# One level of Strassen's algorithm in the up-projections of three feed-forwards

## The chip, the cores and the metric

One NeuronCore of a Trainium2 chip runs the whole program. The metric is device time in microseconds (us). The kernel before takes 2163.91 us (median of 3 runs, 2163.86 to 2165.43).

## The reference, cut to what matters

Three decoder layers run over 512 tokens of 1024 features: a gated linear recurrence (HGRN2), dilated attention, and a sparse attention beside gated linear attention. Each is followed by the same kind of feed-forward, with an inner width of 22 times 128. Everything is float32.

```python
def swiglu_ffn(u, w_in, w_down):
    gate, up = jnp.split(u @ w_in, 2, axis=-1)
    return (jax.nn.silu(gate) * up) @ w_down
...
        h = h + swiglu_ffn(rmsnorm(h, norm_ffn[layer]), ffn_w_in[layer], ffn_w_down[layer])
```

## The kernel before, in words

Activations lie feature-major: a tile is 128 features by 512 tokens. To keep float32 accuracy with fast products, every operand is split into a head (the value rounded to float32r) and a rest (value minus head), and a product of two operands is three matmuls: rest by head, head by head, head by rest (`mm3`, L387). Each matmul loads its own 128x128 stationary weights and streams 512 tokens.

A feed-forward (`ffn`, L1421) runs in two halves of 11 column pairs. A pair is one 128-column tile of the gate matrix and one of the up matrix; `gemm` (L407) makes each tile as 8 blocks of the inner dimension by three matmuls. `evac_up` takes the bank of a gate tile through VectorE (times the norm factor `r_bc`), ScalarE (Silu) and GpSimd (times `r_bc` again), and the bank of an up tile through VectorE (times the gate), ScalarE and VectorE (`split`, L525, into head and rest `h`). After 11 pairs the down-projection runs over those 11 tiles, into 8 output tiles that are added to the residual `x`; then the second half does the same, and in its down-projection `norm_feed` (L449) builds the operands of the next norm.

The norm's factor is computed late: `norm_stats` (L483) and `norm_bc` (L518) wait in a list of hooks, and `tile_end` (L377) runs one of them at each of the first two tile ends of the next product, while `evac` calls are held back.

Weights come as units of 1024 columns (8 blocks). `Weights` (L240) has 3 raw buffers and 3 pairs for heads and rests. `load` (L282) issues a 512 KB DMA on SyncE's queue, `heads` (L262) casts on ScalarE, `rests` (L273) subtracts, on GpSimd for odd units and on VectorE for even ones. `take` (L291) hands blocks to the products, issues heads at 3/8 of a unit and rests at 5/8, so a unit is ready about 1.4 to 1.6 units ahead.

Engines work through their queues in program order, so the order of the calls is the order of the work on each engine. The tile framework gives a new tile a buffer of its pool that was freed earlier, and its first writer waits for the last reader of the tile that held it. `Clock` (L163) only decides where background steps of the mixers are put.

`finish` (L1457) makes the last output tile of the program in two halves of 256 tokens, with the same three matmuls per block, each with its own weights. This is the only long stretch of the kernel before that streams 256 columns per matmul.

Of the kernel before, what the change touches and what calls it, by code (L numbers as in the profile page):

```python
# [17 lines left out]
KD = 8  # L18
FF = 22
# [5 lines left out]
# columns of the packed per-feature vectors  # L25
# [10 lines left out]
# columns of the constants that stay  # L36
# [16 lines left out]
def nsa_rows():  # L53
    """Feature order of the NSA heads: tile j holds head j of group 0 and head j of group 1."""
    return np.concatenate([np.arange((e * 4 + j) * 64, (e * 4 + j) * 64 + 64) for j in range(4) for e in range(2)])


def attn_heads():
    """(head of the group, group) in the order in which the output projection takes them."""
    return [(t, g) for t in range(4) for g in (1, 2)] + [(t, 0) for t in range(4)]  # L60


def weight_plan():
    """The order in which weight blocks are used: (section, [(matrix, k tile, columns)])."""
# [14 lines left out]
    def ffn(name_in, name_down, name_up=None):  # L79
        out = []  # L80
        for half in range(2):
            tiles = []
            for i in range(FH):
                tiles.append(cols((half * FH + i) * 128))
                tiles.append(cols(FF * 128 + (half * FH + i) * 128))
            out += fm(name_in, range(KD), tiles, 2 if half == 0 else 1)
            out += fm(name_down, range(half * FH, half * FH + FH), [cols(m * 128) for m in range(8)], 2)
        return out
# [9 lines left out]
    plan.append(("hgrn", c))  # L98
# [8 lines left out]
    plan.append(("attn", c))  # L107
# [26 lines left out]
    plan.append(("blk2", c))  # L134
# [4 lines left out]
def plan_units(sec, chunks):  # L139
    """Cut a section's blocks into units of at most UNIT columns; the first ones are small, to start early."""  # L140
# [22 lines left out]
class Clock:  # L163
    """Rough times of the engines' queues and of the tiles' contents while the program is laid out:
    they say when a background step's inputs and banks will be there, so that TensorE isn't made to wait."""

    def __init__(self, hop):
        self.hop = hop  # from an instruction's end to the start of another engine's that waits for it
        self.free = {"pe": 0.0, "v": 0.0, "a": 0.0, "g": 0.0}
        self.written, self.read = {}, {}  # L170
        self.held = []
# [4 lines left out]
    def banks(self, now):  # L176
        """PSUM banks that are free by then."""
# [62 lines left out]
class Weights:  # L240
    """Streams the weights in the order of use and splits each into its float32r head and rest."""

    RAW, SPLIT = 3, 3

    def __init__(self, prog, ctx, aps):
        tc = prog.tc
        self.nc, self.v, self.a, self.g = tc.nc, prog.v, prog.a, prog.g
        self.raw_p = ctx.enter_context(tc.tile_pool(name="w_raw", bufs=self.RAW))
        self.sp_p = ctx.enter_context(tc.tile_pool(name="w_split", bufs=self.SPLIT))
        self.units = []  # L250
        for sec, chunks in weight_plan():
            off = 0
            for cur, w in plan_units(sec, chunks):
                ap = aps[sec][off:off + 128 * w].rearrange("(p n) -> p n", p=128)
                self.units.append((ap, [len(c[2]) for c in cur], w))
                off += 128 * w
        self.n_dma = self.n_head = self.n_rest = 0
        self.raw, self.split = {}, {}
        self.at, self.pos, self.idx = 0, 0, 0
        self.look = 1  # L260

    def heads(self, look):  # L262
        while self.n_head < min(self.at + look, len(self.units)):
            u = self.n_head
            self.load(u + 1)
            w = self.units[u][2]
            hi = self.sp_p.tile([128, UNIT], F32R, name="w_hi", tag="w_hi")
            lo = self.sp_p.tile([128, UNIT], F32R, name="w_lo", tag="w_lo")
            self.a.copy(hi[:, :w], self.raw[u][:, :w])
            self.split[u] = (hi, lo)  # L270
            self.n_head += 1

    def rests(self):  # L273
        while self.n_rest < self.n_head:
            u = self.n_rest
            w = self.units[u][2]
            hi, lo = self.split[u]
            (self.g if u % 2 else self.v).tensor_sub(lo[:, :w], self.raw.pop(u)[:, :w], hi[:, :w].bitcast(F32))
            self.n_rest += 1
        self.load(self.n_rest + self.RAW - 1)  # L280

    def load(self, n):  # L282
        while self.n_dma < min(n, len(self.units)):
            u = self.n_dma
            ap, _, w = self.units[u]
            raw = self.raw_p.tile([128, UNIT], F32, name="w_raw", tag="w_raw")
            self.nc.sync.dma_start(raw[:, :w], ap)
            self.raw[u] = raw
            self.n_dma += 1

    def take(self, n):  # L291
        ap, widths, w = self.units[self.at]
        if self.idx == 0:
            self.split.pop(self.at - 1, None)
            if self.at not in self.split:
                self.heads(1)
                self.rests()
        if self.idx == 3 * len(widths) // 8:
            self.heads(self.look)
        if self.idx == 5 * len(widths) // 8:  # L300
            self.rests()
        assert widths[self.idx] == n, (self.at, self.idx, widths, n)
        hi, lo = self.split[self.at]
# [3 lines left out]
        if self.idx == len(widths):  # L307
            self.at, self.idx, self.pos = self.at + 1, 0, 0
        return r


class Program:
# [74 lines left out]
    def mm3(self, out, a, b, first, last):  # L387
        """out += a^T b for operands given as (head, rest)."""
# [18 lines left out]
    def gemm(self, xs, M, evac, lead=1, ms=None):  # L407
# [15 lines left out]
    def gemm_tok(self, n, residue=False, before=None, after=None, every=1):  # L423
        """Token-major product with n weight columns: four banks of 128 tokens, by blocks or by the rest of the token mod 4."""
# [24 lines left out]
    def norm_feed(self, k, squares=True):  # L449
        """x[k] is final: build the operand's parts and add its squares."""  # L450
# [25 lines left out]
    def sums(self, out, acc, residue=False):  # L476
        """Each token's sum over the partitions of acc, onto the token's partition."""
# [1174 lines left out]
```

## Time and profile before

| | |
|---|---|
| median of 3 runs | 2163.91 us |
| profiled execution, span of its instructions | 2162.1 us |
| profiled execution, own time | span and about 1.8 us around it, 2163.9 us |
| mean granted TensorE clock | 0.994 of full speed |
| TensorE busy | 2117.4 us, 98% of the span |
| VectorE, ScalarE, GpSimd busy | 46%, 36%, 33% |
| DMA, mean | 88 GB/s |

A profile line gives the start in us, the duration, the engine (PE is TensorE, PEld its weight loads, DVE VectorE, ACT ScalarE, POOL GpSimd, SP SyncE), the operation and its tiles as out<-in. Nearly all operations are recorded at line L228, the timing wrapper, so groups are told apart by tile names. Busy spans of PE overlap, since matmuls are pipelined: the pace of a stretch is read from the distance of starts. "[... <-X]" is idle time of the engine just before and what ended it.

### The profile page before, as it was taken

Reading aid. Unit: us, or ns where it says so; the run is one execution under the profiler, and the core shown is the slowest. Engines: PE = TensorE matmul, PEld = TensorE weight load, DVE = VectorE, ACT = ScalarE, POOL = GpSimd, SP = SyncE. Lnnn points to the kernel's source line nnn. Section 1 sums busy time; section 2 is a strip of 40 time slices with the busy share of each in tenths; the row PEclk is TensorE's granted clock in tenths of the full one; section 3 lists DMA queues with packets and bytes.
Section 4 is the critical chain, followed back from the end, with each engine's and each line's share of the span. In section 5 each row is a group of like instructions: output and inputs, shape, how many; then the busy total and the mean of one; then the engine's idle time right before and its main releaser. Section 6 shows DMA issues by size and latency. Waiting matters only on the chain.

```text
span 2162.1 us, 25412 instructions
## 1 busy us (share of the span) xinstructions
PE 2117.4 (98%) x9983; PEld 1773.4 (82%) x9983; DVE 1004.3 (46%) x1775; ACT 783.8 (36%) x1290; POOL 723.6 (33%) x442
## 2 busy tenths in 40 slices
PE   9999999999999999999999999999899999999998
PEld 7787788888888998788888888887688788888887
DVE  4778853322334555643322333447778753222322
ACT  5343443222233433443222224244455543222233
POOL 4413343323333434323322335331511253322333
PEclk9999999999999999999999999999999999999999
DMA  5111233323323222222332232321111223333332
GB/s 178 59 59 49 69 127 98 98 98 98 98 88 107 79 88 78 79 69 98 98 102 93 98 98 92 133 69 48 55 55 57 70 95 98 98 98 98 96 100 69
DMA packets 55865, 191.00 MB, mean 88 GB/s; under 512 B 6257, under 2 KB 8321, under 8 KB 55745
## 3 DMA queue, kind: packets, MB, share of 16 engines
q1 hardware_dynamic: 53584, 183.85, 26.2%
q0 software_dynamic: 1008, 3.42, 0.4%
q10 hardware_dynamic: 1152, 2.10, 0.3%
q8 instruction: 78, 1.28, 0.2%
q14 instruction: 43, 0.34, 0.1%
HBM read 187.25 MB, written 2.10 MB: 88 GB/s over the span
## 4 chain that ended last, share of the span: by engine, by line
PE 86%; DVE 9%; issue 1%; POOL 1%; ACT 1%; DMA 1%; SPq 0%; DVEq 0%; ACTq 0%; POOLq 0%
PE ps L228 86%; DVE Q L228 2%; DVE Sd L228 2%; DVE P L228 1%; DMA w_raw<-in_hgrn 1%; DVE w_lo L228 1%; DVE K L228 0%; POOL rot L228 0%; DVE Pc L228 0%; DVE qs L228 0%; POOL rs L228 0%; DVE obl L228 0%; DVE GQ L228 0%; DVE PT L228 0%; POOL w_lo L228 0%
## 5 line engine op out<-in xcount | busy, mean ns | idle before, releaser
L228 PE MATMUL ps<-u,w_hi 128*128 128x512 f32 x3392 | 1049.4, 391 | 0.0
L228 PEld LDWEIGHTS ps<-u,w_hi 128*128 128x128 f32 x3392 | 638.9, 188 | 128.9 <-issue 1.4
L228 PE MATMUL ps<-u,w_lo 128*128 128x512 f32 x1696 | 683.7, 403 | 2.2 <-POOL w_lo L228 2.2
L228 POOL TENSOR_TENSOR w_lo<-w_raw,w_hi 128x1024 fp32r<-128x1024 f32 (+2 forms) x173 | 415.8, 2403 | 745.1 <-ACT w_hi L228 636.2
L228 ACT CAST w_hi<-w_raw 128x1024 fp32r<-128x1024 f32 (+2 forms) x346 | 356.1, 1030 | 301.6 <-PE ps L228 205.4
L228 PEld LDWEIGHTS ps<-u,w_lo 128*128 128x128 f32 x1696 | 319.7, 189 | 68.3 <-issue 4.2
L228 PE MATMUL ps<-h,w_hi 128*128 128x512 f32 (+1 forms) x1078 | 326.3, 385 | 0.0
L228 DVE TENSOR_TENSOR w_lo<-w_raw,w_hi 128x1024 fp32r<-128x1024 f32 (+2 forms) x173 | 231.5, 1338 | 183.7 <-ACT w_hi L228 175.4
L228 PEld LDWEIGHTS ps<-h,w_hi 128*128 128x128 f32 x1078 | 200.9, 188 | 40.4
L228 PE MATMUL ps<-h,w_lo 128*128 128x512 f32 (+1 forms) x539 | 207.6, 385 | 0.5 <-DVE x L228 0.5
L228 POOL TENSOR_TENSOR sg<-sg,r_bc 128x512 f32<-128x512 f32 x66 | 85.8, 1299 | 290.3 <-ACT sg L228 290.3
L228 DVE TENSOR_TENSOR x<-x,ps 128x512 f32<-128x512 f32 (+1 forms) x73 | 49.5, 678 | 218.6 <-PE ps L228 218.6
L228 PE MATMUL ps<-w_hi,u 128*128 128x512 f32 (+1 forms) x448 | 139.1, 392 | 2.3 <-DVE u L228 2.3
L228 DVE TENSOR_TENSOR h<-ps,sg 128x512 f32<-128x512 f32 x66 | 45.7, 692 | 194.9 <-PE ps L228 182.4
L228 ACT ACTIVATE sg<-gs 128x512 f32<-128x512 f32 x66 | 41.7, 632 | 242.3 <-DVE gs L228 242.3
L228 ACT CAST h<-h 128x512 fp32r<-128x512 f32 x66 | 41.0, 620 | 242.8 <-DVE h L228 242.8
L228 DVE TENSOR_TENSOR gs<-ps,r_bc 128x512 f32<-128x512 f32 x66 | 45.6, 691 | 156.8 <-PE ps L228 156.7
L228 PEld LDWEIGHTS ps<-h,w_lo 128*128 128x128 f32 x539 | 101.2, 188 | 20.9 <-DVE x L228 0.7
L228 ACT ACTIVATE P<-P,nm 128x128 f32<-128x128 f32 (+2 forms) x112 | 55.2, 494 | 142.6 <-DVE nm L228 130.4
L228 POOL TENSOR_TENSOR sq_acc<-sq_acc,sq 128x512 f32<-128x512 f32 x48 | 67.2, 1405 | 117.8 <-ACT sq L228 115.7
L228 PEld LDWEIGHTS ps<-w_hi,u 128*128 128x128 f32 x448 | 95.0, 226 | 10.3 <-DVE u L228 2.7
L228 PE MATMUL ps<-w_lo,u 128*128 128x512 f32 (+1 forms) x224 | 85.8, 383 | 0.0
(294 smaller groups left out, 2231.5 us busy)
## 6 DMA issues: line engine op xcount, KB each, us to landing
w_raw<-in_ffn SPq DMA_DIRECT2D x198, 512.0 KB, 3.5
w_raw<-in_attn SPq DMA_DIRECT2D x48, 512.0 KB, 3.5
w_raw<-in_blk SPq DMA_DIRECT2D x47, 512.0 KB, 3.4
w_raw<-in_hgrn SPq DMA_DIRECT2D x36, 512.0 KB, 3.5
w_raw<-in_blk SPq DMA_DIRECT2D x7, 404.0 KB, 2.9
x<-in_xt SPq DMA_DIRECT2D x8, 256.0 KB, 5.1
w_raw<-in_hgrn SPq DMA_DIRECT2D x8, 256.0 KB, 4.0
x<-in_xt ACTq DMA_DIRECT2D x8, 256.0 KB, 5.0
```

What stands on the lines that cost most here:

```text
L228: r = f(*args, **kw)
```

## The change

In each feed-forward the first 5 column pairs (FC) are made as before; the other 17 by one level of Strassen's algorithm (6 in the first half, 11 in the second). The 2x2 blocks are: the inner dimension in even and odd k tiles, the columns in gate and up tile, the tokens in two halves of 256. Seven products a1, b1, a2, b2, c, a3, a4 replace eight; each is 4 inner blocks by three matmuls of 256 columns. Their order interleaves neighbouring pairs: a4 of a pair comes after a1 and b1 of the next.

Of the activations, `strassen_operands` makes sums and splits for two k tiles at a time, four times in a feed-forward, during the first 5 pairs (VectorE and ScalarE). Of the weights, each pair needs four sums of 512 columns on VectorE, heads on ScalarE and rests on VectorE; two of the rests (half of the third tile and that of a4) are made by ScalarE writing the negated head and a GpSimd-issued DMA adding the weights to it from memory. All weight tiles share one pool of 12 buffers of 4 KB. Ordinary units get the heads 8.8 and the rests 7.5 us ahead by a planned clock; in the feed-forwards their rests are all on VectorE. The two norm hooks run at k = 4 and 6 of the first group of tiles. The scratch for software DMA descriptors goes from the default to 4096 bytes.

```diff
+FC = 5
+REST = {"hgrn": "vg", "ffn0": "v", "attn": "vg", "ffn1": "v", "blk2": "vg", "ffn2": "v"}
+S_AT = {"a1": 0, "b1": 1, "a2": 3, "b2": 4, "c": 5, "a3": 6, "a4": 9}
+S_LAST = {"a1": 0, "b1": 1, "a2": 3, "b2": 4, "a3": 5, "c": 6, "a4": 7}
+def strassen_order(n):
+    at = [(7 * g + t, g, p) for g in range(n) for p, t in (S_AT if g < n - 1 else S_LAST).items()]
+    return [(g, p) for _, g, p in sorted(at)]
...
-    RAW, SPLIT = 3, 3
+    ROOM, HELD = 12, 3
+    TILE, SLOT = 0.68, 1.44
...
+        self.pool = ctx.enter_context(tc.tile_pool(name="w", bufs=self.ROOM))
...
+    def rest_dma(self, lo, hi, ap):
+        self.a.activation(lo, hi.bitcast(F32), AF.Copy, scale=-1.0)
+        self.nc.gpsimd.dma_start(lo, ap, accum_op=ALU.add)
+
+    def group(self, grp):
...
+        def sums_1():
+            add("r1", second, "r4", second, "r4", first)
+            add("r3", second, "r1", first, "r4", second)
+        def sums_2():
+            t["r2"] = self.tile(F32)
+            add("r2", first, "r1", first, "r1", second)
+            add("r2", second, "r3", first, "r2", first)
+        def heads(i):
+            def go():
+                t["h%d" % i] = self.tile()
+                self.a.copy(t["h%d" % i][:, :2 * n], t["r%d" % i][:, :2 * n])
...
+        def rests(i):
+            def go():
+                h, l = t["h%d" % i], self.tile()
...
+                if i == 3:
+                    self.rest_dma(l[:, first], h[:, first], aps[2])
+                    self.sub(v, l[:, second], t["r3"][:, second], h[:, second])
+                else:
+                    self.sub(v, l[:, :2 * n], t["r%d" % i][:, :2 * n], h[:, :2 * n])
+                self.free(t, "r%d" % i)
...
+        def last():
+            t["l4"] = self.tile()
+            hi, lo = t["l4"][:, second], t["l4"][:, first]
+            self.a.copy(hi, t["r4"][:, first])
+            self.rest_dma(lo, hi, aps[0][:, first])
...
+        for use, lead, what in (
+            ("a1", 7, sums_1), ("a1", 6, sums_2), ("a1", 5, heads(1)), ("a1", 4, rests(1)), ("a2", 6, heads(2)), ("a2", 5, rests(2)),
+            ("c", 6, heads(3)), ("c", 5.9, rests(3)), ("a1", 0, last),
+        ):
+            self.todo.append((at[use] - lead * s + 0.01, u, what, len(self.loads)))
...
+            while self.n_load < len(self.loads) and self.live < self.ROOM - self.HELD:
+                self.load(self.n_load + 1)
...
+                if grp[0] == 0 and k in hooks_at:
+                    self.hooks.popleft()()
...
+    def strassen_operands(self, k, gain):
+        B1, B2, t13, t24 = [self.s2("E", (128, 2, 256)) for _ in range(4)]
+        for B, i in ((B1, k), (B2, k + 1)):
+            v.scalar_tensor_tensor(
+                B.rearrange("p a n -> p (a n)"), self.x[i], gain[:, i:i + 1], self.r_bc, op0=ALU.mult, op1=ALU.mult)
+        v.tensor_sub(t13[:, 0], B1[:, 0], B1[:, 1])
+        v.tensor_sub(t13[:, 1], B2[:, 1], B1[:, 1])
+        v.scalar_tensor_tensor(t24[:, 0], t13[:, 0], -1.0, B2[:, 1], op0=ALU.mult, op1=ALU.subtract)
+        v.scalar_tensor_tensor(t24[:, 1], t24[:, 0], -1.0, B2[:, 0], op0=ALU.mult, op1=ALU.subtract)
+        for src, names in ((B1[:, 0:1], ("a1",)), (t13, ("b1", "a3")), (B2, ("c", "b2")), (t24, ("a2", "a4"))):
...
+            a.copy(P[:, 0], src)
+            v.tensor_sub(P[:, 1], src, P[:, 0].bitcast(F32))
...
+            if i in (1, 2, 4, 6):
+                X.append(self.strassen_operands(2 * len(X), self.V[inner]))
...
+            def c(ps):
+                v.tensor_add(gt[:, n1], gt[:, n1], ps)
+                a.activation(gt[:, n1], gt[:, n1], AF.Silu)
+            def b2(ps):
+                v.tensor_add(gt[:, n2], gt[:, n2], ps)
+                a.activation(gt[:, n2], gt[:, n2], AF.Silu)
+            def a3(ps):
+                v.tensor_add(f[:, n2], f[:, n2], ps)
+                v.scalar_tensor_tensor(f[:, n2], f[:, n2], -1.0, gt[:, n2], op0=ALU.mult, op1=ALU.mult)
+            def a4(ps):
+                v.scalar_tensor_tensor(f[:, n1], ps, -1.0, gt[:, n1], op0=ALU.mult, op1=ALU.mult)
+                hh[i] = self.split(f, "h")
+            return {
+                "a1": lambda ps: a.copy(gt[:, n1], ps), "b1": lambda ps: a.copy(f[:, n2], ps),
+                "a2": lambda ps: a.copy(gt[:, n2], ps), "b2": b2, "c": c, "a3": a3, "a4": a4,
...
-    nc = bacc.Bacc("TRN2", target_bir_lowering=False, num_devices=1)
+    nc = bacc.Bacc("TRN2", target_bir_lowering=False, num_devices=1, dynamic_dma_scratch_size=4096)
```

## Rows read from the trace of the kernel before

**Rows 1.** The page's head and its busy time of each engine.

```profile
span 2162.1 us, 25412 instructions
...
PE 2117.4 (98%) x9983; PEld 1773.4 (82%) x9983; DVE 1004.3 (46%) x1775; ACT 783.8 (36%) x1290; POOL 723.6 (33%) x442
```

**Rows 2.** The chain of work that ended last, by engine.

```profile
PE 86%; DVE 9%; issue 1%; POOL 1%; ACT 1%; DMA 1%; SPq 0%; DVEq 0%; ACTq 0%; POOLq 0%
```

**Rows 3.** Busy time in stretches: the first feed-forward's up, down, up, down.

```profile
core 0: us, PE busy (x) PEld busy (x) DVE busy (x) ACT busy (x) POOL busy (x), PEclk, DMA share, GB/s
319.00:439.60 120.60, 120.60 (x537) 99.76 (x536) 39.07 (x48) 38.27 (x48) 41.63 (x23) 1.00 0.30 96
439.60:499.50 59.90, 59.90 (x266) 49.57 (x265) 13.36 (x15) 12.12 (x12) 11.97 (x5) 1.00 0.32 105
499.50:619.20 119.70, 119.70 (x530) 99.12 (x529) 38.50 (x43) 34.07 (x43) 40.61 (x22) 1.00 0.29 93
619.20:679.00 59.80, 59.80 (x266) 49.51 (x265) 20.17 (x21) 20.39 (x26) 24.02 (x13) 1.00 0.30 95
```

**Rows 4.** Timeline of PE at the program's end: 512, then 256 columns per matmul.

```profile
2140.81 0.39 PE L228 MATMUL ps<-h,w_lo 128*128 128x512 f32 x1
...
2141.49 0.39 PE L228 MATMUL ps<-h,w_lo 128*128 128x512 f32 x1
...
2142.88 0.28 PE L228 MATMUL ps<-h,w_lo 128*128 128x256 f32 x1
...
2143.24 0.28 PE L228 MATMUL ps<-h,w_lo 128*128 128x256 f32 x1
```

**Rows 5.** Groups by shape on DVE and ACT, whole span: busy, mean ns.

```profile
L228 DVE SCALAR_TENSOR_TENSOR x<-x,vec,ps 128x512 f32<-128x512 f32 x8 | 5.6, 741 | 0.0
...
L228 DVE TENSOR_TENSOR x<-x,ps 128x256 f32<-128x256 f32 x2 | 0.8, 420 | 3.9 <-PE ps L228 3.9
...
L228 ACT ACTIVATE sq<-x 128x256 f32<-128x256 f32 x2 | 0.8, 417 | 3.8 <-DVE x L228 3.8
...
L228 ACT COPY r_bc<-ps 128x256 f32<-128x256 f32 x2 | 0.7, 373 | 2.2 <-PE ps L228 2.2
```

**Rows 6.** Groups by shape in one up-projection, 499.5 to 619.2 us.

```profile
L228 ACT CAST w_hi<-w_raw 128x1024 fp32r<-128x1024 f32 x22 | 22.9, 1040 | 4.3 <-PE ps L228 4.3
L228 DVE TENSOR_TENSOR w_lo<-w_raw,w_hi 128x1024 fp32r<-128x1024 f32 x11 | 16.4, 1487 | 18.0 <-ACT w_hi L228 18.0
...
L228 DVE TENSOR_TENSOR gs<-ps,r_bc 128x512 f32<-128x512 f32 x11 | 7.6, 692 | 37.7 <-PE ps L228 37.7
...
L228 DVE TENSOR_TENSOR h<-h 128x512 fp32r<-128x512 f32 x10 | 6.9, 693 | 6.9 <-ACT h L228 6.9
...
L228 ACT CAST h<-h 128x512 fp32r<-128x512 f32 x10 | 6.2, 620 | 39.4 <-DVE h L228 39.4
```

**Rows 7.** Timeline of the same stretch: a rest on DVE beside POOL, and alone.

```profile
604.47 1.30 POOL L228 TENSOR_TENSOR sg<-sg,r_bc 128x512 f32<-128x512 f32 x1 [1.98 <-ACT sg L228]
605.36 1.49 DVE L228 TENSOR_TENSOR w_lo<-w_raw,w_hi 128x1024 fp32r<-128x1024 f32 x1 [1.64 <-ACT w_hi L228]
...
625.92 1.22 DVE L228 TENSOR_TENSOR w_lo<-w_raw,w_hi 128x1024 fp32r<-128x1024 f32 x1 [4.43 <-ACT w_hi L228]
```

**Rows 8.** DMA issues, whole span: size, median us from issue to landing.

```profile
w_raw<-in_ffn SPq DMA_DIRECT2D x198, 512.0 KB, 3.5
...
tab<-in_rope POOLq DMA_DIRECT2D x2, 256.0 KB, 4.6
...
cosr<-in_rope POOLq DMA_DIRECT2D x1, 256.0 KB, 5.2
```

**Rows 9.** DMA issues from 1350 to 1370 us, where both queues are busy.

```profile
w<-in_w POOLq DMA_DIRECT2D x4, 512.0 KB, 7.9
w_raw<-in_blk SPq DMA_DIRECT2D x2, 512.0 KB, 5.8
```

**Rows 10.** Timeline of DVE and ACT in the norm hooks of the first feed-forward.

```profile
330.48 0.69 DVE L228 TENSOR_REDUCE st<-ps 128x4 f32<-128x512 f32 x1 [7.15 <-PE ps L228]
331.53 0.18 DVE L228 RECIPROCAL r<-rt 128x4 f32<-128x4 f32 x1 [0.36 <-ACT rt L228]
...
331.20 0.30 ACT L228 ACTIVATE rt<-st,eps 128x4 f32<-128x4 f32 x1 [4.21 <-DVE st L228]
```

More of the change, by code (lines that the diff above doesn't have):

```diff
@@ new lines, in __init__, with plain, load, heads @@
+        self.todo.sort(key=lambda x: x[0])
+        self.n_todo = self.n_load = 0
+        self.at, self.pos, self.idx, self.now = 0, 0, 0, 0.0
+        self.look = 1
+    def plain(self, ap, widths, w, use, rest):
+        unit = {"ap": ap, "widths": widths, "w": w, "use": use}
+        u = len(self.units)
+        self.units.append(("c", unit, None))
+        def load():
+            unit["raw"] = self.tile(F32)
+            self.nc.sync.dma_start(unit["raw"][:, :w], ap)
+        def heads():
+            unit["hi"] = self.tile()
+            self.a.copy(unit["hi"][:, :w], unit["raw"][:, :w])
+        def rests():
+            unit["lo"] = self.tile()
+            hi, lo = unit["hi"][:, :w], unit["lo"][:, :w]
+            if rest == "d":
+                self.rest_dma(lo, hi, ap)
+            else:
+                self.sub(self.g if rest == "g" else self.v, lo, unit["raw"][:, :w], hi)
+            self.free(unit, "raw")
+        self.loads.append([load, u])
+        self.todo.append((use - 8.8, u, heads, len(self.loads)))
+        self.todo.append((use - 7.5, u, rests, len(self.loads)))
@@ new lines, in tile, with free, advance @@
+    def tile(self, dt=F32R):
+        self.live += 1
+        assert self.live <= self.ROOM, (self.at, self.now)
+        return self.pool.tile([128, UNIT], dt, name="w_raw" if dt == F32 else "w", tag="w")
+    def free(self, tiles, *names):
+        for n in names:
+            del tiles[n]
+            self.live -= 1
+    def load(self, n):
+        while self.n_load < min(n, len(self.loads)):
+            self.loads[self.n_load][0]()
+            self.n_load += 1
+    def advance(self):
+        while self.n_todo < len(self.todo):
+            due, u, what, n = self.todo[self.n_todo]
+            if due > self.now or (self.look == 1 and u > self.at):
+                break
+            self.load(n)
+            what()
+            self.n_todo += 1
+        if self.look > 1:
+            while self.n_load < len(self.loads) and self.live < self.ROOM - self.HELD:
+                self.load(self.n_load + 1)
@@ L304, in take @@
+    def take(self, n):
+        _, unit, _ = self.units[self.at]
+        self.now = max(self.now, unit["use"] + self.pos / 128 * self.TILE)
+        self.advance()
+        hi, lo = unit["hi"], unit["lo"]
+        assert unit["widths"][self.idx] == n
         r = hi[:, self.pos:self.pos + n], lo[:, self.pos:self.pos + n]
@@ L306, in take, with product @@
         self.pos += n
-        if self.idx == len(widths):
+        if self.idx == len(unit["widths"]):
             self.at, self.idx, self.pos = self.at + 1, 0, 0
+            self.free(unit, "hi", "lo")
+        return r
+    def product(self, p):
+        _, grp, name = self.units[self.at]
+        assert p == name, (self.at, p, name)
+        self.now = grp["at"][p]
+        self.advance()
+        r = grp["split"].pop(p)
+        self.at += 1
+        if p in ("b1", "b2", "a3", "a4"):
+            self.free(grp["tiles"], *{"b1": ("l1", "h1"), "b2": ("l2", "h2"), "a3": ("l3", "h3"), "a4": ("l4",)}[p])
         return r
@@ new lines, in strassen @@
+    def strassen(self, X, afters):
+        banks = {}
+        for g, p in strassen_order(len(afters)):
+            key = g, p[0]
+            first = key not in banks
+            if first:
+                banks[key] = self.ps((128, 256))
+            hi, lo = self.W.product(p)
+            for j in range(len(X)):
+                sl = slice(128 * j, 128 * j + 128)
+                self.mm3(banks[key], (hi[:, sl], lo[:, sl]), X[j][p], first and j == 0, j == len(X) - 1)
+            afters[g][p](banks[key])
@@ L1450, in ffn @@
             last = half == 1 and not operands
-            self.gemm(hh, 7 if last else 8, evac_dn, lead=2)
+            self.gemm(hh[mine], 7 if last else 8, evac_dn, lead=2)
+            if not last:
+                hh[mine] = [None] * FH
         if last:
-            self.finish(hh)
+            self.finish(hh[mine])
         else:
```

198 lines of the change are left out of this document (114 added, 84 removed).

## The prediction

> **What bounds the kernel now.** I read the page's head first: of a span of 2162.1 us TensorE is busy 98%, the other engines 33 to 46% [rows 1]. The chain that ended last agrees: 86% of it is PE, 9% DVE, everything else 1% or less [rows 2]. So the first question is how much TensorE time goes, and the second whether the helpers can still feed it. The change sits in the feed-forwards, so I read the first one by stretches: up 120.6, down 59.9, up 119.7, down 59.8 us, 360.0 in all. In each PE is busy for the whole stretch at a granted clock of 1.00, the level of 2.4 GHz [rows 3]. DVE works 38.5 of the 119.7 us of an up-projection there, ACT 34.1, POOL 40.6: a third each, with two thirds idle to be filled.
>
> PE's pace I read from starts, since busy spans overlap. In the timeline of the program's end three matmuls of 512 columns go by from 2140.81 to 2141.49, 0.68 us, and three of 256 columns from 2142.88 to 2143.24, 0.36 us [rows 4]. Each has its own 128x128 weights in both cases. A matmul of half the columns costs 0.120 us, 53% of 0.227.
>
> **PE's term.** A pair takes 16 blocks before (2 tiles of 8), 16 x 0.68 = 10.88 us; 11 pairs make 119.7, which is the stretch [rows 3]. After it takes 7 products of 4 inner blocks, 28 x 0.36 = 10.08 us. That is 0.80 saved, not the 1.36 of an eighth, because of the 53%. Three feed-forwards have 51 such pairs: **-40.8 us**, if PE never waits for its operands. Unchanged are the down-projections, the 5 plain pairs (5 x 10.88 = 54.4 us), the mixers.
>
> One rule of the Trainium skill gives another size. Its page "TensorE: Matmul & The Clock Gate", section "Back-to-back issue gap", has 109 ns for 256 columns and 216 ns for 512. By these a pair would go from 10.37 to 9.17 us, -61 us in 51 pairs. The rows' 120 and 227 ns decide; no row here shows 109.
>
> **What it asks of the other engines.** Per Strassen pair, 10.08 us of PE:
> - DVE: four sums of 512 columns, priced by the two-operand subtraction of a split, 0.69 [rows 6]: 2.76. Rests: two of 1024 columns at 1.22, the time without POOL beside it [rows 7], and half of one, 0.69: 3.13. Evacuation: five operations on 256 columns at 0.42 [rows 5] and the rest of the split, 0.69: 2.79. In all **8.7 us, 86%**.
> - ACT: three heads of 1024 at 1.04 and three half-size operations (one negation for l3, head and negation for a4, 256 columns each, 0.37): 4.2. Evacuation: three copies at 0.37, two Silus at 0.42 (priced as the square), one head of the split 0.62 [rows 5, 6]: 2.6. In all **6.8 us, 67%**.
> - POOL only issues the adding DMAs. The two multiplications by `r_bc` of a pair and its share of the rests are gone from it.
> - DMA: 1024 KB per pair as before, plus two adding DMAs that read 256 KB each again, so half as much again on a share of 0.30 [rows 3]. Mean bandwidth is no bound.
>
> So the engines fit by their sums, but DVE only by 1.4 us per pair, and queues are in order: what counts is the chains that cross between them.
>
> **The first 5 pairs.** In these 54.4 us DVE has the gate and up evacuation of 5 pairs, 5 x (0.69 + 0.74 + 0.69) = 10.6; all 10 or 11 rests, x 1.22 = 13.4; four times `strassen_operands`: 2 x 0.74 to scale, 4 x 0.42 for the sums, about 0.42 + 3 x 0.69 for the rests, 5.2, so 21; the sums and rests of the first Strassen pairs about 6; the hooks' 2 [rows 5, 6, 7, 10]. Some 53 of 54.4 us: nearly full, so now and then late. Bounds: 0, if the 7.5 us of lead take it all, and 6 us a feed-forward, one `strassen_operands` with its hop, that PE waits in full. I take 1 us each, nearer to the lower end since weight rests lead: **+3** (0 to 18).
>
> **The chain of the weights.** A pair's own chain runs through three queues. Load of r4 3.5 us [rows 8], four sums 2.8, then on DVE and ACT in turn heads and rests for tiles 1 to 3, with the evacuations of earlier products queued between them: `c`'s and `b2`'s adds and Silus, a4's 0.42, the split. If each step finds its engine free it starts 7 slots of 1.44 us ahead of a1 and all is hidden. It does not always: an add that waits for a bank stands before the next rest, and the rest for ACT's head. I add up the order in which one pair's steps stand: a4's add 0.42, split head 0.62, head 1.04, rest 1.22, b2's add 0.42, Silu 0.42, head 1.04, rest 1.22, four sums 2.76, about **9.2 us**. That is inside 10.08, spare 0.9. The trace of before has no such loop, so I bound its waits by these rows: 0 per pair, if it turns inside 10.08; about 2.5, if a load of 3.5 comes into it (below). I take 0.35, nearer to the lower end, since the loop without a load fits: 0.35 x 51 = **+18**.
>
> **The adding DMAs.** No row has one. The nearest are plain POOL-queue loads of 256 KB, 4.6 and 5.2 us to landing [rows 8], and 512 KB ones where both queues are busy, 7.9, beside which a 512 KB SP load takes 5.8 in place of 3.5 [rows 9]. The tight one is the third tile's for `c`: its head is due 6 products (8.64 us) before `c`, behind the Silu of the pair before. Add and Silu 0.84, head 1.04, negation 0.37 to 0.62, hops 0.2, then 4.6 to 5.2: 7.1 to 7.9 us, hidden with some 0.7 to 1.5 to spare. With 7.9 to landing it is 10.4, PE waits about 2 us in each pair. An accumulation also reads its target, so below the plain load it can't be, above it can. I take 5, **0**; both ends stay in the range. A page of the Trainium skill, "DMA: Bandwidth & Descriptors", section "Anatomy of one DMA — SWDGE", prices such a transfer at 2.0 us and its bytes at 436 GB/s, 2.6 us by my estimate; the rows' 4.6 and 5.2 stand against it, and by either the term is 0.
>
> **The rest.** Rests only on DVE take nothing from PE in the plain stretches: 1.22 against a unit of 5.4 us (8 x 0.68). The hooks at k = 4 and 6 are two inner blocks of two tiles apart, 4 x 0.68 = 2.7 us; the chain between them is reduce 0.69, root 0.30, reciprocal 0.18 with hops, 330.48 to 331.71 [rows 10]: **0**. The heads' and rests' new leads (8.8 and 7.5 us) in the mixers are about the 1.4 to 1.6 units of before: **0**; bounds one rest of 1.2 us sooner or later in each of the three mixers, -4 to +4.
>
> **Sum.** Profiled execution: span 2162.1 and 1.8 around it, 2163.9, as the median of 2163.91. 2163.9 - 40.8 + 3 + 18 + 0 = **2144 us**.
>
> **The rivals.**
> *All hidden.* Loop and DMAs stay inside 10.08 us: 2123, with small stage losses 2118 to 2130. For it: sums of 86 and 67%, a loop of 9.2. Against: 0.9 us of spare over three in-order queues. Chance 0.24.
> *A load in the loop (slower).* All weight tiles share 12 buffers, so r4's load, the first of a pair, waits for whatever buffer was freed first. If that is the one of r2, freed by the second rest of the pair before, the load's 3.5 us stand in the loop: 9.2 + 3.5 = 12.7, or 2.6 more than PE needs, in some 45 pairs +117, 2164 - 41 + 117 = 2240. It decides from 0.8 us of wait a pair upward: there the whole saving is gone. Where only half of it shows, 2180 to 2200. Against: heads and rests read by PE are freed earlier in part. Chance 0.15.
> *The adding DMA lands late (slower).* At 7.9 us, +2 x 51 = +102 on 2123: 2225; at 7.0, about +1 x 51: 2174. Chance 0.14.
> *The matmuls don't shrink.* If weights did not load under 256 columns, a matmul would take twice its 0.12. [rows 4] has them back to back with own weights, so 2 x 84 x 0.12 = 20.2 us a pair, +9.3 x 51 = +474, 2638: chance 0.01. The Trainium skill ("TensorE: Matmul & The Clock Gate", section "LDWEIGHTS") has a load at 107 ns for 128 columns; this row shows it hidden.
> *No change within 0.2%* (2159.6 to 2168.2, about what a measurement of this kernel can tell): waits of 0.8 a pair by chance: 0.08.
>
> **How the numbers follow.** Forecast, waits of 0.1 to 0.7 us a pair, 2130 to 2159: 0.38. With all hidden, 0.24: faster 0.62. Same 0.08. Slower 0.15 + 0.14 + 0.01 = 0.30. The likeliest case's own range is 2130 to 2159; to hold 8 in 10 it reaches down to 2119 and up to 2195, which leaves out the upper half of the slower cases.
>
> **What would show it.** In the second Strassen stretch of a feed-forward (11 pairs) the profile should take 111 us if PE never waits, 115 by my forecast, 120 at break-even, 139 with a load in the loop. Starts of 256-column matmuls 0.12 us apart; DVE 85% busy, ACT 67%, POOL near 0. Idle PE before `a1` or `a2` ended by a rest on DVE shows the loop; before `c` or `a4`, ended by a DMA, the adding ones; waits of SP on a buffer before r4's load, the pool. It is wrong if the stretch takes 111 and the time still doesn't fall (then the plain pairs lose it), or if 256-column matmuls start further apart than 0.12 with nothing to wait for.

## The result and the profile after

The changed kernel takes **2247.84 us** (median of 4 runs, 2243.74 to 2255.88) against 2164.43 before on the same chip: a ratio of 1.0391 (95% interval 1.0371 to 1.0410). It is slower by 83 us; the forecast was 2144 and the range ended at 2195.

The page's head and busy times, to be held against [rows 1]:

```profile
span 2242.0 us, 30605 instructions
...
PE 2114.1 (94%) x11819; PEld 1844.4 (82%) x11819; DVE 1358.9 (61%) x2402; ACT 999.9 (45%) x1750; POOL 507.0 (23%) x394
```

The span is 79.9 us longer, while PE's busy time is about what it was (2117.4). No engine became full: DVE went from 46% to 61%. So PE waits. Where, the windows of the first feed-forward tell, cut as in [rows 3] but with the up-projection's plain and Strassen pairs apart; the last line is the end of the second Strassen stretch alone:

```profile
core 0: us, PE busy (x) PEld busy (x) DVE busy (x) ACT busy (x) POOL busy (x), PEclk, DMA share, GB/s
319.40:378.07 58.67, 56.43 (x249) 45.41 (x248) 47.87 (x73) 27.25 (x40) 7.87 (x5) 1.00 0.19 59
378.07:456.25 78.18, 66.27 (x505) 64.84 (x505) 48.22 (x75) 41.29 (x73) 11.61 (x13) 0.94 0.58 145
456.25:516.18 59.93, 59.93 (x266) 49.64 (x265) 23.39 (x27) 13.69 (x14) 0.86 (x1) 1.00 0.25 72
516.18:644.84 128.66, 115.84 (x926) 113.30 (x925) 84.49 (x135) 72.61 (x129) 18.21 (x21) 0.97 0.61 146
644.84:704.70 59.86, 59.86 (x266) 49.55 (x265) 25.87 (x26) 20.05 (x26) 11.69 (x9) 1.00 0.31 100
640.10:644.84 4.74, 4.74 (x25) 4.74 (x26) 1.56 (x2) 0.42 (x1) 0.00 (x0) 0.58 0.30 88
```

The down-projections are as before. Six Strassen pairs take 78.18 us where PE needs 60.5 (6 x 10.08), eleven take 128.66 where it needs 110.9; before, eleven pairs took 119.7. The three feed-forwards together are 73.8 us longer, the three mixers 6.1.

What PE waited for in the whole span (us in total, times, longest), the first lines:

```profile
PE ps L249 <- DMA w<-in_ffn: 57.8, 39, 6.8
PE ps L249 <- ACT G L249: 15.0, 12, 2.6
```

And the timeline of PE in the second stretch:

```profile
568.06 10.46 PE L249 MATMUL ps<-E,w 128*128 128x256 f32 x84 [0.48 <-DMA w<-in_ffn]
579.23 10.33 PE L249 MATMUL ps<-E,w 128*128 128x256 f32 x84 [0.71 <-DMA w<-in_ffn]
...
622.79 11.81 PE L249 MATMUL ps<-E,w 128*128 128x256 f32 x96 [0.64 <-DMA w<-in_ffn]
640.10 4.90 PE L249 MATMUL ps<-E,w 128*128 128x256 f32 x24 [5.50 <-DMA w<-in_ffn]
644.84 1.55 PE L249 MATMUL ps<-h,w 128*128 128x512 f32 x6
```

Two things are to be seen. In the **middle**, PE runs 84 matmuls (one pair) and then waits half a microsecond for an adding DMA, pair after pair: 10.8 to 11.2 us from one start to the next, against 10.88 for a plain pair. So the whole saving is gone. At the **end** of the stretch it waits 5.50 us, and the last 24 matmuls (c and a4) then take 4.74 us in place of 2.88: the granted clock there is 0.58, between the levels of 2.4 and 1.2 GHz (1.00 and 0.50), while the pairs of the middle, 568.06 to 622.79 us, ran at 1.00. All six stretches end so: waits of 5.5 to 6.8 us, 36.2 in all, and then 4.5 to 5.3 us for the last 24 matmuls, 12.4 more than at full clock.

The profile names the DMA as the releaser. Whether it is the cause is another question: what comes last is not always what sets the pace. By the prediction's own list of signs (idle PE before `c`, ended by a DMA) it would be the adding DMAs.

### The profile page after: what moved, and what is told of

It reads as the page before. It is cut to its first block, busy times and chain, and to the rows that moved or that the text cites. A ratio compares the mean times of both kernels' runs of the same rounds, so it can differ in the third digit from the quotient of the medians.

```text
span 2242.0 us, 30605 instructions
## 1 busy us (share of the span) xinstructions
PE 2114.1 (94%) x11819; PEld 1844.4 (82%) x11819; DVE 1358.9 (61%) x2402; ACT 999.9 (45%) x1750; POOL 507.0 (23%) x394
## 5 line engine op out<-in xcount | busy, mean ns | idle before, releaser
L249 PE MATMUL ps<-u,w 128*128 128x512 f32 x2640 | 664.3, 401 | 8.1 <-DVE w L249 7.3
L249 PE MATMUL ps<-E,w 128*128 128x256 f32 x4284 | 546.8, 290 | 74.6 <-DMA w<-in_ffn 57.8
L249 PEld LDWEIGHTS ps<-E,w 128*128 128x128 f32 x4284 | 534.0, 197 | 88.0 <-DMA w<-in_ffn 66.3
L249 PEld LDWEIGHTS ps<-u,w 128*128 128x128 f32 x2640 | 485.7, 189 | 111.9 <-DVE w L249 10.7
L249 ACT CAST w<-w_raw 128x1024 fp32r<-128x1024 f32 (+2 forms) x448 | 438.5, 984 | 224.6 <-DVE w L249 113.4
L249 DVE TENSOR_TENSOR w<-w_raw,w 128x1024 fp32r<-128x1024 f32 (+2 forms) x323 | 386.9, 1200 | 205.9 <-ACT w L249 158.9
L249 PE MATMUL ps<-h,w 128*128 128x512 f32 (+1 forms) x1617 | 361.6, 385 | 0.5 <-DVE x L249 0.5
L249 PEld LDWEIGHTS ps<-h,w 128*128 128x128 f32 x1617 | 299.4, 188 | 60.9 <-DVE x L249 0.7
L249 POOL TENSOR_TENSOR w<-w_raw,w 128x1024 fp32r<-128x1024 f32 (+3 forms) x74 | 176.3, 2383 | 371.8 <-ACT w L249 288.7
L249 DVE TENSOR_TENSOR w_raw<-w_raw 128x512 f32<-128x512 f32 x204 | 135.5, 688 | 49.2 <-DMA w_raw<-in_ffn 47.6
L249 PE MATMUL ps<-w,u 128*128 128x512 f32 (+1 forms) x672 | 156.7, 389 | 1.8 <-DVE u L249 1.8
```

What stands on the lines that cost most here:

```text
L249: r = f(*args, **kw)
```

## The experiments

The first four took the adding DMAs away, all or in part, since theory A (the adding DMAs are the loss) is what the list of waits says.

**Both by POOL (e1), c's alone (e2), a4's alone (e3).** e1 has both edits, e2 the first, e3 the second:

```diff
-                    self.rest_dma(l[:, first], h[:, first], aps[2])
+                    self.sub(self.g, l[:, first], t["r3"][:, first], h[:, first])
...
-            self.rest_dma(lo, hi, aps[0][:, first])
+            self.sub(self.g, lo, t["r4"][:, first], hi)
```

> Both adding DMAs of a pair (the third tile's for c, and a4's) become a subtraction on POOL; nothing else changes. Theory A (the adding DMAs are the loss: each pair c waits for its own, and at the end of each half two of them meet the loads of the down-projection): the 57.8 us that PE waits for DMA w go, and with them the low clock behind the long waits, some 20 us. Time 2165 (2155 to 2178); stretch of 11 Strassen pairs 112 to 116 us in place of 128.7. Rival B (the loop over DVE and ACT is too long by itself, or a load waits for a buffer in it): the DMA waits turn into waits for DVE w or ACT w, stretch 122 to 128, time 2215 to 2248. Rival C (POOL beside DVE slows DVE, rests of 1.22 become 1.49): stretch 116 to 120, time 2175 to 2200.

> Only c's adding DMA becomes a subtraction on POOL; a4's stays a DMA. Theory A, with the loss in c's loop: the waits in the middle of a stretch (0.5 to 0.7 us a pair) go, and at the end of a half a4's DMA alone lands 1 to 2 us late: time 2175 (2165 to 2190). Rival A2 (the queue is simply overloaded, any adding DMA makes waits): 2200 to 2230. Rival B: 2215 to 2248.

> Only a4's adding DMA becomes a subtraction on POOL; c's stays a DMA. Theory A, with the loss in c's loop: the steady waits stay at 0.4 to 0.7 a pair, and at the ends c's DMA is alone in its queue and lands 2 to 3 us earlier: time 2230 (2215 to 2240). Rival A2 (two transfers crowd the queue): half or more of the loss goes, 2180 to 2205. Rival B: 2240 to 2248.

Measured: e1 2223.51 (1.0277, 1.0262 to 1.0293), e2 2206.99 (1.0199, 1.0182 to 1.0216), e3 2235.37 (1.0334, 1.0319 to 1.0350). Without any adding DMA the kernel (e1) is still 60 us slower than before, so theory A alone fell; the time is in rival B's range. e2 was a miss for theory A too: its time is in the range of rival A2, but not for A2's reason, since PE's waits for a DMA are down to 6.5 us and it waits 42.2 us for ACT's G. e3 came out as theory A said: c's waits stay (44.1 us for DMA w), the ends get shorter. e1 is worse than e2 for a reason of its own, in its timeline:

```profile
567.47 2.73 POOL L249 TENSOR_TENSOR w<-w_raw,w 128x512 fp32r<-128x512 f32 x2 [9.33 <-DVE w L249]
567.56 0.62 ACT L249 CAST w<-w_raw 128x512 fp32r<-128x512 f32 x1
567.75 1.28 DVE L249 SCALAR_TENSOR_TENSOR h<-h,G 128x256 f32<-128x256 f32 x1
...
568.96 1.78 DVE L249 TENSOR_TENSOR w<-w_raw,w 128x512 fp32r<-128x512 f32 x1
```

While POOL subtracts, DVE's product of 256 columns takes 1.28 us (0.42 alone) and its half rest 1.78 (0.69 alone). The two subtractions on POOL cost DVE 0.86 + 1.09 = 1.95 us; done by DVE itself they would have cost 2 x 0.69 = 1.38 by these rows. The Trainium skill ("SBUF — State Buffer", section "Who interferes with whom") says that a DVE instruction with two SBUF inputs contends with a GpSimd instruction that reads SBUF, and these lines agree.

**Only the last pair of each half (e4).** `end` marks the last group of a stretch; there both rests go to POOL:

```diff
+                    grp["end"] = grp is groups[-1]
...
-                    self.rest_dma(l[:, first], h[:, first], aps[2])
+                    if grp["end"]:
+                        self.sub(self.g, l[:, first], t["r3"][:, first], h[:, first])
+                    else:
+                        self.rest_dma(l[:, first], h[:, first], aps[2])
...
-            self.rest_dma(lo, hi, aps[0][:, first])
+            if grp["end"]:
+                self.sub(self.g, lo, t["r4"][:, first], hi)
+            else:
+                self.rest_dma(lo, hi, aps[0][:, first])
```

> Both adding DMAs become POOL subtractions in the last pair of each half alone, six pairs of 51. Theory A, split by place: the six waits of 5.5 to 6.8 us go and the low clock behind them (2 to 2.5 us each), 6 x 8 = 48: time 2198 (2190 to 2208), and the middle of the stretches stays at 10.9 us a pair. If the loss were spread evenly over the pairs (rival B, or the pace of the matmuls): -10 at most, 2235 to 2248.

Measured 2198.74 (1.0162, 1.0147 to 1.0177), the 2198 expected: six ends cost 49 us, 8.2 each, which is the wait and the slow matmuls counted above (36.2 + 12.4 = 48.6). The rest of the loss lies elsewhere.

**All by DVE (e8), and c's by DVE with the last a4's (e10).** e8 takes both edits; e10 the first, and the second only where `end` (set as in e4) is true.

```diff
-                if i == 3:
-                    self.rest_dma(l[:, first], h[:, first], aps[2])
-                    self.sub(v, l[:, second], t["r3"][:, second], h[:, second])
-                else:
-                    self.sub(v, l[:, :2 * n], t["r%d" % i][:, :2 * n], h[:, :2 * n])
+                self.sub(v, l[:, :2 * n], t["r%d" % i][:, :2 * n], h[:, :2 * n])
...
-            self.rest_dma(lo, hi, aps[0][:, first])
+            self.sub(v, lo, t["r4"][:, first], hi)
```

> Both adding DMAs of all pairs become VectorE's (the third tile's rest in one operation of 1024 columns, 1.22 in place of 0.69; a4's 0.69); ScalarE loses both negations. Theory A: no wait for a DMA is left, and VectorE has 8.7 + 0.53 + 0.69 = 9.9 us per pair of 10.08: stretch of 11 pairs 113 to 117, time 2172 (2165 to 2185). Rival D (VectorE and ScalarE wait for each other in turn, so that 9.9 of work doesn't fit): stretch 120 to 128, time 2190 to 2225, PE waiting for ACT G.

> The third tile's rest wholly on VectorE (1.22), a4's rest by DMA as in the changed kernel, except in the last pair of each half, where it is VectorE's too. Theory A: a4's DMA has 9 slots and is hidden; no wait for a DMA; VectorE 9.2 us per pair: stretch 112 to 115, time 2168 (2162 to 2180). Rival D: stretch 117 to 125, 2185 to 2215, PE waiting for ACT G.

Measured 2195.29 (1.0148, 1.0133 to 1.0163) and 2186.19 (1.0106, 1.0091 to 1.0121). No wait for an adding DMA is left in either, and eleven pairs still take 118 to 122 us: rival D. PE's waits are now named differently (43.8 us for ACT G in e8, 33.5 in e10) at the same 11 us per pair. So there is a loop of about the same length without an adding DMA in it.

**The third tile earlier (e9).** One line:

```diff
-            ("c", 6, heads(3)), ("c", 5.9, rests(3)), ("a1", 0, last),
+            ("c", 7.1, heads(3)), ("c", 7.05, rests(3)), ("a1", 0, last),
```

> From the changed kernel only the leads of the third tile's head and rest go from 6 and 5.9 to 7.1 and 7.05 slots, so that in ScalarE's queue the head and the negation stand ahead of the Silu of the pair before's c, and the DMA no longer hangs on that c. Theory A (c to c by way of Silu, head, negation and DMA is a loop of 10.9 us): the middle of the stretches falls to 10.1 to 10.4 a pair, the ends stay: 45 x 0.6 = 27 less, 2220 (2212 to 2232). Rival A2 (the transfers land late because the queue is busy, not because they start late): 2240 to 2250. Rival D: the wait turns into one for DVE or ACT, 2240 to 2260.

Measured 2262.62 (1.0461, 1.0445 to 1.0477), a miss: slower still. Its list of waits:

```profile
PE ps L249 <- DVE h L249: 44.9, 35, 1.6
PE ps L249 <- ACT G L249: 36.9, 26, 3.1
PE ps L249 <- DMA w<-in_ffn: 15.9, 10, 3.1
```

The waits for the DMA fell from 57.8 to 15.9 us, as meant, and nothing was gained: DVE's half rest now stands in front of c's add and waits 2.37 us for ScalarE's head. This run put in a wait of its own, so it does not yet say what the DMA's late landing cost in the middle; e14 does.

**No Strassen (e5).** The one pool, the leads, the hooks and the rests on DVE stay, all 22 pairs are plain:

```diff
-            out.append(("s", [(name_in, ks, *up[i]) for i in range(FH * half if half else FC, FH * half + FH)]))
+            out.append(("c", fm(name_in, range(KD), [c for t in up[FH * half if half else FC:FH * half + FH] for c in t])))
...
-            if i in (1, 2, 4, 6):
-                X.append(self.strassen_operands(2 * len(X), self.V[inner]))
...
-            self.strassen(X, [lazy(i) for i in range(FH * half if half else FC, FH * half + FH)])
+            o = FH * half if half else FC
+            self.gemm(self.u, 2 * (FH * half + FH - o), lambda i, ps, o=o: evac_up(i + 2 * o, ps))
...
```

> All 22 pairs of each feed-forward as plain products (16 blocks of 512 columns), no operands, sums or adding DMAs; the one pool of 12 buffers, the planned leads, the hooks at k = 4 and 6 and the plain rests on VectorE stay. Theory A (Strassen's operands and adding DMAs hold the loss; what came with them is small): the feed-forwards take 360 us as before, the mixers keep the 5.6 us that the last one lost: 2170 (2164 to 2173). Rival E (the pool or the leads cost the feed-forwards too): 363 to 370 each, 2175 to 2195.

Measured 2169.28 (1.0031, 1.0020 to 1.0042): theory A's 2170. What came along with Strassen costs the feed-forwards nothing (360.0 us for the first, as before) and the mixers about 6 us. In the trace nearly all of it lies in the third mixer (443.1 us in place of 437.5); which of the leads or of the pool does it was not tried.

**The second loop.** In the timelines of DVE and ACT in the changed kernel one period of the middle reads so (other lines left out):

```profile
561.39 1.23 DVE L249 TENSOR_TENSOR w<-w_raw,w 128x1024 fp32r<-128x1024 f32 x1 [1.09 <-ACT w L249]
...
565.36 2.02 DVE L249 TENSOR_TENSOR w_raw<-w_raw 128x512 f32<-128x512 f32 x3 [0.76 <-DMA w_raw<-in_ffn]
567.30 0.42 DVE L249 SCALAR_TENSOR_TENSOR h<-ps,G 128x256 f32<-128x256 f32 x1
567.75 0.62 ACT L249 CAST h<-h 128x512 fp32r<-128x512 f32 x1 [2.77 <-DVE h L249]
...
568.28 1.05 ACT L249 CAST w<-w_raw 128x1024 fp32r<-128x1024 f32 x1
...
569.36 1.23 DVE L249 TENSOR_TENSOR w<-w_raw,w 128x1024 fp32r<-128x1024 f32 x1 [0.26 <-ACT w L249]
570.50 0.74 DVE L249 TENSOR_TENSOR G<-G,ps 128x256 f32<-128x256 f32 x2
570.95 0.42 ACT L249 ACTIVATE G<-G 128x256 f32<-128x256 f32 x1 [1.36 <-DVE G L249]
571.27 1.03 ACT L249 CAST w<-w_raw 128x1024 fp32r<-128x1024 f32 x1
...
572.34 1.23 DVE L249 TENSOR_TENSOR w<-w_raw,w 128x1024 fp32r<-128x1024 f32 x1 [1.09 <-ACT w L249]
```

Rest 2 of a pair ends at 561.39 + 1.23 = 562.62. SyncE's queue, seen alone, issues a load of 256 KB at 562.64:

```profile
562.64 0.33 SPq L348 DMA_DIRECT2D w_raw<-in_ffn  x1
```

It lands 2.6 us later, and at 565.36 DVE's sums start, released by it. Then a4's operation, the split's head, head 1, rest 1, the first of the two adds (b2's), Silu, head 2, and rest 2 of the next pair ends at 573.57: 10.95 us. That is the pace of the stretch, and no adding DMA stands in it. Rest 2 is the last reader of the tile r2, so the reading is that the load waits for r2's buffer; e14 tests it. In e8 DVE's four sums start without a wait at the same place, since its added rests fill the time that the load took here (DVE waits for loads 6.5 us in e8, 19.4 in e10, 47.6 here). There the loop is closed by DVE's own queue and ScalarE. Two ways to open such a loop: move a step of it, or give it a buffer.

**Moving the split (e11, e12, e13).** The split of a pair's output is issued after b2's evacuation in the next pair:

```diff
+        late = []
+
+        def splits():
+            while late:
+                i, f = late.pop()
+                hh[i] = self.split(f, "h")
...
                 a.activation(gt[:, n2], gt[:, n2], AF.Silu)
+                splits()
...
-                hh[i] = self.split(f, "h")
+                late.append((i, f))
+                if i % FH == FH - 1:
+                    splits()
```

e11 has this alone, e12 on top of e10, e13 with c's rest of the last pairs on POOL and a4's on DVE.

> From the changed kernel only one thing moves: the split of a pair's output (head on ScalarE, rest on VectorE) is issued behind b2's evacuation of the next pair and not behind a4's, so that ScalarE's next weight head and a2's copy no longer stand behind a head that waits for VectorE's sums and a4. Theory F (there are two loops of about 11 us a pair, that of c's adding DMA and that of VectorE and ScalarE by way of sums, a4, split head, weight head 1, rest 1, Silu, head 2, rest 2; the second one is also in the first, since c's add stands behind rest 1): the middle of the stretches falls from 10.9 to 10.2 to 10.5 a pair, the six ends stay: 2222 (2212 to 2236). Rival A (the DMA's loop alone, whatever stands ahead): 2240 to 2250.

> The late split on top of c's rest on VectorE and, in the last pairs, a4's too (the run of 2186 us). Theory F: both loops are open and nothing waits for a DMA; stretches of 11 pairs 111 to 113 us in place of 118 to 120, of 6 pairs 63 to 65 in place of 67 to 69: 2186 - 3 x 13 = 2147 (2139 to 2160), faster than the kernel before. Rival G (VectorE with 9.2 us of 10.08 is the bound, in whatever order): 2172 to 2188.

> The late split on top of the changed kernel with its adding DMAs, except in the last pair of each half (c's on POOL, a4's on VectorE). Theory F: the DMA of c starts about 0.6 us earlier in the loop and lands in time: 2198.7 - 3 x (9 + 4) = 2160 (2148 to 2175). Rival A: c still waits for its DMA 0.3 to 0.7 in each pair: 2180 to 2199.

Measured: e11 2250.00 (1.0398, 1.0382 to 1.0415), e13 2199.43 (1.0166, 1.0150 to 1.0183), each as without the move; e12 2157.59 (0.9974, 0.9965 to 0.9984), faster than the kernel before and in theory F's range, with 112 to 113 us for eleven pairs. By e11 and e13 theory F was wrong where the adding DMAs stay. Their traces say why: DVE there waits for loads, 91.0 us in e11, 96.6 in e13, 47.6 in the changed kernel; the line of e13:

```profile
DVE w_raw L249 <- DMA w_raw<-in_ffn: 96.6, 57, 4.4
```

The step taken out of the loop became a longer wait for the load. In e12 that wait is 33.0 us in all, and in the second stretch PE stops twice, for 0.70 and 0.51 us. Why the move pays there and not in e11 and e13 was not taken further.

**A buffer more (e14).** The work tiles of 4 KB go from 26 to 25 to make room for it:

```diff
-    ROOM, HELD = 12, 3
+    ROOM, HELD = 13, 3
...
-        self.p4 = ctx.enter_context(tc.tile_pool(name="p4", bufs=26))
+        self.p4 = ctx.enter_context(tc.tile_pool(name="p4", bufs=25))
```

> The changed kernel with 13 in place of 12 weight buffers (and 25 in place of 26 of the 4 KB work tiles); nothing else. Rival P (a load that waits for a buffer stands in the loop; VectorE waits 0.7 us a pair for a load): the middle falls by 0.4 to 0.7 a pair, 2215 to 2232. Theory F (the loops don't hang on buffers): 2240 to 2252.

Measured **2200.45** (1.0166, 1.0148 to 1.0184), 47 us less, beyond rival P's own range. DVE's waits for loads in the changed kernel and in e14:

```profile
DVE w_raw L249 <- DMA w_raw<-in_ffn: 47.6, 52, 2.7
DVE w_raw L249 <- DMA w_raw<-in_ffn: 0.6, 2, 0.3
```

The loads moved by one buffer: r1's is issued at 566.67, as rest 2 starts (566.70), and the one that is issued as rest 2 ends (567.93) is r3's, at 567.95. PE's timeline of the second stretch is

```profile
507.68 86.55 PE L249 MATMUL ps<-E,w 128*128 128x256 f32 x720
594.75 21.85 PE L249 MATMUL ps<-E,w 128*128 128x256 f32 x180 [0.52 <-DMA w<-in_ffn]
622.01 5.49 PE L249 MATMUL ps<-E,w 128*128 128x256 f32 x24 [5.41 <-DMA w<-in_ffn]
```

Seven hundred matmuls without a gap, 0.12 us each, with every adding DMA of the middle still there: once they start in time, they are hidden, but for 0.52 us. So in the middle their late landing was a symptom. Only the end is left.

**Both mends (e15).** 13 buffers as in e14, and in the last pair of each half both rests by DVE. **The ends, split (e18):** the same without the first edit, so that c's rest of the last pair stays a DMA.

```diff
-                    self.rest_dma(l[:, first], h[:, first], aps[2])
+                    if grp["end"]:
+                        self.sub(v, l[:, first], t["r3"][:, first], h[:, first])
+                    else:
+                        self.rest_dma(l[:, first], h[:, first], aps[2])
...
-            self.rest_dma(lo, hi, aps[0][:, first])
+            if grp["end"]:
+                self.sub(v, lo, t["r4"][:, first], hi)
+            else:
+                self.rest_dma(lo, hi, aps[0][:, first])
```

> The changed kernel with 13 weight buffers (25 of the 4 KB work tiles) and, in the last pair of each half alone, both half rests by VectorE in place of adding DMAs; 45 pairs keep their adding DMAs. Theory H (two losses that add: the first loads of a pair wait for the buffer that the pair before's rest 2 frees, which makes a loop of 10.9 us, and at the six ends two adding DMAs meet the loads of the down-projection): 2200.5 - 6 x 8 = 2152 (2146 to 2160), faster than the kernel before; stretches of 11 pairs 111 to 113. If the two overlap (the ends are shorter only because the middle was late): 2165 to 2185. If the adding DMAs cost by themselves in the middle: over 2170 with waits for DMA w there.

> 13 buffers; in the last pair of each half only a4's rest is VectorE's, c's stays an adding DMA. If the 5 to 6 us at the ends come from two adding DMAs at once: c's lands about 5 us after its issue, the wait falls to 1 or 2 and the low clock mostly goes, 2160 to 2175. If they come from the loads of the down-projection beside it, or from c's late start: 2185 to 2200.

e15 takes **2149.75** (0.9938, 0.9923 to 0.9953), 13.6 us faster than the kernel before: theory H. 98.1 us are gained on the changed kernel, 49.1 (e4, there with POOL for the two rests) and 47.4 (e14) by the two mends one by one: they add up. Its windows:

```profile
318.65:377.29 58.64, 56.44 (x249) 45.41 (x247) 47.84 (x73) 27.27 (x40) 7.86 (x5) 1.00 0.17 54
377.29:440.56 63.27, 60.84 (x505) 60.64 (x506) 48.83 (x77) 40.51 (x71) 9.86 (x11) 1.00 0.62 163
440.56:500.42 59.86, 59.86 (x266) 49.58 (x265) 23.62 (x28) 13.68 (x14) 0.87 (x1) 1.00 0.24 77
500.42:611.43 111.01, 111.01 (x925) 110.93 (x924) 85.44 (x137) 72.44 (x127) 16.41 (x19) 1.00 0.65 166
```

The second stretch takes 111.01 us: PE's term (11 x 10.08 = 110.9) to 0.1, at a granted clock of 1.00, with DVE 77% and ACT 65% busy.

e18 takes 2166.37 (1.0021, 1.0011 to 1.0030), in the range for two DMAs at once. PE's waits for adding DMAs fall from 36.5 us in all (e14) to 12.3. In the last pair of a half a4's DMA is issued first (ScalarE's copy and negation for it stand ahead of c's negation), and c, which PE needs first, has the second one. At the end of the changed kernel's second stretch the two landed after 7.2 and 9.2 us (below with their median), beside loads of the down-projection:

```profile
w_raw<-in_ffn SPq DMA_DIRECT2D x2, 512.0 KB, 7.8
w<-in_ffn POOLq DMA_DIRECT2D x2, 256.0 KB, 8.2
```

c's alone, in e18, landed after 7.0 beside the loads of the down-projection, against 3.9 to 5.4 for c's in the middle of that stretch. So the end has both causes: the neighbours on the DMA engines, some 2 to 3 us, and standing as the second transfer behind the first, another 2.

**Further (e16, e17).** e16 is e12 with 13 buffers as in e14; e17 also moves the operand steps:

```diff
-            if i in (1, 2, 4, 6):
+            if i in (1, 3, 5, 7):
```

> 13 weight buffers on top of the best run so far (c's rest on VectorE, a4's of the last pairs too, late split; 2157.6). Theory H: that run had no waits left in the middle, so a buffer more brings only what the start of the first stretch loses, 0 to 4: 2155 (2150 to 2159). Rival (the buffers still bound it): below 2150.

> As the run before it, with the four operand steps of a feed-forward behind tiles 1, 3, 5 and 7 in place of 1, 2, 4 and 6, so that two of them don't stand in a row on VectorE in front of a weight rest. If the 1.6 us wait for a rest in the plain pairs comes from that row: 2 to 3 less in each feed-forward, 2148 (2143 to 2153). If the last operands then come too late for the first product: 2155 to 2170.

Measured 2153.52 (0.9959, 0.9945 to 0.9973), theory H's 2155, and 2155.38 (0.9967, 0.9954 to 0.9980). In e17 the wait for a weight rest inside the plain pairs falls from 1.6 us to 0.4 and 0.5, and PE waits 3.7 us before the first product instead. The time is in the range of e17's second alternative, but what PE waits for is DVE's weights and not the operands. There is no gain, and e15 stays the best.

## Why the prediction was wrong, step by step

**PE's term, -40.8 us: right.** 0.120 us per matmul and 10.08 per pair stand in e15 as worked out. No run shows 109 ns. The Trainium skill ("TensorE: Matmul & The Clock Gate", section "Back-to-back issue gap") gives its 109 and 216 ns for a single matmul by itself, which the prediction did not say.

**The chain of the weights, +18: the step that failed.** I added up a loop of 9.2 us and took 0.35 of wait per pair. In this loop I had left out the load: it stood in the rival "a load in the loop", with a chance of 0.15. That rival had the right mechanism (a load that takes the buffer that rest 2 frees) and two wrong details: the load is r1's 256 KB (2.6 us), not r4's 512 KB, and with it only three of the four sums stand in the chain. So the period is 10.95, not 12.7: 2.74 from the end of rest 2 to the sums, and 8.21 for the steps that are left of my 9.2. The price in the middle measured 47 us (e14), where I had 117 for the rival and 18 for the forecast. The pool's buffers were never counted through a pair in the prediction, so nothing in it could tell which of the two would come.

**The adding DMAs, 0: right in the middle, wrong at the ends; the second step that failed.** In the changed kernel's second stretch the twenty ahead of the last pair land after 3.6 to 6.8 us, with a median of 5.0, and they are hidden as soon as the load is (e14). The prediction's lower bound, no less than a plain load's 4.6, doesn't hold: the shortest took 3.6. At the ends of the six stretches they cost 49 us (e4), a place that the prediction doesn't have. [rows 9] had the size: beside transfers of the other queue a 512 KB load takes 5.8 us instead of 3.5. The prediction used it for the steady loop alone. In the last pair the DMAs of a4 and c start together, and the next stage's loads start just then. 6 us of wait there also cost 2 us of clock each time, a term that was missing.

**The negations: a slip.** I counted the two negations and a4's head as 256 columns, 0.37 us; they are 512, and took 0.62 to 0.63. ACT then has 7.6 us of work per pair by the rows' prices, not 6.8. It changed nothing: ACT was 56% busy in the second stretch, 72.61 of 128.66, or 6.6 per pair.

**The first five pairs, +3: too low.** In e15, where the two large losses are gone, the plain stretch takes 58.64 us where some 55.3 are needed (5 x 10.88 and about 0.9 for the hooks) and the first Strassen stretch 63.27 for 60.48: 6.1 per feed-forward, 18 in all. That is the upper end that I gave (0 to 18). The sum had a slip: by its own prices one `strassen_operands` is 1.48 + 1.68 + 2.49 = 5.65 us, not 5.2, so DVE's total is 54.6 of 54.4 us and not 53: there was no room at all. In e15 the last three of the first feed-forward take 6.0 to 6.1 us each, and DVE is 82% busy. Of the 6.1, PE's waits show 4.5: 1.63 for a weight rest queued behind operand steps, 0.47 for the first Strassen weights, and 2.43 before the third product, where ScalarE's copy of the first bank stands behind a split that waits for DVE. e17 shortened the first and lengthened the second; no run removed them.

**The mixers, 0 (-4 to +4):** +6 (e5), nearly all in the third.

Together: -40.8 + 47 + 49 + 18 + 6 = +79. The spans of the profiled executions differ by 79.9, but the medians, from which the 47 and 49 come, by 83: some 4 us are in no term. With only the first, fourth and fifth terms it would have been 2147, and e15 took 2149.75. The two terms that decided were waits, not work: DVE's busy time per pair was forecast at 8.7 us and is 7.8 in e15 (85.44 over 11 pairs; instructions that follow each other without a wait overlap a little).

## What to carry to other kernels

Before a pool of shared buffers is trusted, count which release each load waits for; if it is a late step of the item before, the load's latency is part of the period. One more buffer was worth 47 us here, more than the arithmetic saved. And the wait that the profile names last can be a symptom when the thing waited for started late: follow its start back one period before removing it, and look at the last item of each stretch by itself.

## What the hardware showed beyond this

An idle PE is paid for twice, but not always. After the six waits of 5.5 to 6.8 us the next two products ran at granted clocks of 0.50 to 0.61, 4.5 to 5.3 us in place of 2.88. After shorter waits it went both ways: behind the same wait of 2.4 us before the third product of the first stretch the next 3 us ran at 1.00 in e15 and at 0.63 in e18, and behind 2.69 us at the end of e18's second stretch at 0.67. So these runs give a price, and no length below which a wait is free of it.

An adding DMA of 256 KB took 3.6 to 10.6 us from issue to landing in the changed kernel, with a median of 4.9 over all 102, about as much as the plain ones of [rows 8]. The Trainium skill's figure ("DMA: Bandwidth & Descriptors", section "Anatomy of one DMA — SWDGE"), 2.6 us by the prediction's estimate, is below every one of them.
